# Expert weights in a two-layer mixture-of-experts kernel: 2 MB loads into 16 KB places for six of the eight pairs of experts in each layer

## The chip, the cores and the metric

One core of one Trainium2 chip. The metric is device time in microseconds (us) of one execution. The engines are PE (TensorE, matmul), DVE (VectorE), ACT (ScalarE), POOL (GpSimd) and SP (SyncE, which here only issues transfers); sixteen DMA engines move data between device memory and SBUF. All engines run their own instruction streams in order and wait for one another by semaphores.

## The reference

A first block (a conformer convolution and an MLP) is followed by a second block of two layers. Each of these two layers ends with an expert-choice mixture of experts, and the change is there alone:

```python
def ec_moe(h, w_router, w_gate, w_up, w_down):
    b, n, d = h.shape                                 # 1, 512, 1024
    cap = EC_CAPACITY_FACTOR * n // N_EXPERTS         # 64 tokens for each of 16 experts
    aff = jax.nn.softmax(h.astype(jnp.float32) @ w_router.astype(jnp.float32), axis=-1)
    g, idx = lax.top_k(aff.swapaxes(1, 2), cap)
    xs = jax.vmap(lambda hb, ib: hb[ib])(h, idx)
    a = jax.nn.silu(jnp.einsum('becd,edf->becf', xs, w_gate)) * jnp.einsum('becd,edf->becf', xs, w_up)
    y = jnp.einsum('becf,efd->becd', a, w_down) * g[..., None].astype(h.dtype)
    ...  # the rows of y are added back at the tokens idx
```

Each expert has three 1024 x 1024 float32 matrices (gate, up, down) of 4 MB. Sixteen experts in two layers make 403 MB that have to be read once.

## The kernel before

The kernel is written in a tile language: a program names tiles in pools, and a scheduler derives every semaphore wait from which instruction reads and writes which tile. A pool is a stretch of SBUF; a tile of a tag that has n buffers takes the n buffers in turn, and what writes a buffer waits until the last reader of its former tile is done.

`moe(l)` runs once for each layer. It treats the sixteen experts in eight pairs (j and j + 8, j = 0 to 7): expert j uses the left 64 columns of the PE array and expert j + 8 the right 64. For a pair, `gate_up` makes the gate product and the up product by `product` (L1465), the activation lies between and behind them on ACT and DVE, and `down` transposes the activation, makes the down product and adds the result to the 512 tokens (`combine`, L1534, in layer 0; `add_rows`, L1545, in layer 1). Between these, `gather` and `gather_part` (L1427) pick the next pair's tokens by matmul. From the first pair's down part on, PE's order is held as written.

A product has eight k steps; each takes four matmuls (two halves of 512 columns for each of two experts, L1473). The weights of a step come from a load. `rows` views a matrix as `(p k) n -> p k n`, so that partition p holds rows 8p to 8p + 7, which lie in one run of device memory; two k steps are then 8 KB in one run for each partition, 1 MB over 128 partitions. `product` asks `eload` for such a load for each expert at every second k step, which makes 8 loads to a product and 24 (25.17 million bytes) to a pair. SP issues all of them, in program order, and an SP instruction that waits holds up all loads behind it.

`eplace` gives the SBUF place of a load, from a ring of 14 places of 8 KB a partition: eight pages of the pool `wst` ("p"; tile name w), and the halves of three big buffers, b0, b1 and b3 ("0", "1", "3"; in layer 1 the tensor X stands in for b3). A half-buffer pair is one tile. Two more loads of the first pair go to small tiles (`we`). A place is loaded again when PE has done the products of its former load.

```python
place = "wlwh"[2 * self.ng - 28:2 * self.ng - 26] if self.ng in (14, 15) else \
    "pppppppp001133"[(self.ng - 2 * (self.ng > 15)) % 14]
```

The scheduler gives SP's loads eight completion semaphores in turn (DMAHW0 to DMAHW7), and a load waits until the load before it on its semaphore has landed: at most eight loads are under way.

For the last pair (j = 7), `down_last` (L1560) reads the down matrices in two halves of 512 columns, in loads of 512 KB whose runs are 2 KB (512 float32), so that the first half of the output can be finished while the second is read.

Of the kernel before, what the change touches and what calls it, by code (L numbers as in the profile page):

```python
# [5 lines left out]
F32 = mybir.dt.float32  # L6
# [5 lines left out]
PSUM = bass.MemoryType.PSUM  # L12
# [141 lines left out]
class _Net:  # L154
# [8 lines left out]

    def run(self):
        tc = self.tc
        with tc.tile_pool(name="per", bufs=1) as self.per, \
                tc.tile_pool(name="wst", bufs=8) as self.wst, \
                tc.tile_pool(name="wsp", bufs=4) as self.wsp, \
                tc.tile_pool(name="big", bufs=1) as self.big, \
                tc.tile_pool(name="tmp", bufs=2) as self.tmp, \  # L170
                tc.tile_pool(name="sml", bufs=2) as self.sml, \
                tc.tile_pool(name="dram", bufs=1, space=bass.MemoryType.DRAM) as self.dram:
            self.setup()
            with tc.tile_pool(name="ps", bufs=1, space=PSUM) as self.ps:
                self.block1()
                if self.stop >= 4:
                    self.layer0_proj()
            if self.stop >= 5:
                with tc.tile_pool(name="ps", bufs=1, space=PSUM) as self.ps:
                    self.layer0_attn()  # L180
            with tc.tile_pool(name="ps", bufs=1, space=PSUM) as self.ps:
                if self.stop >= 6:
                    self.mix_out(0, self.a["w_out"], self.oh, self.ol, "gm", last_head=True)
                if self.stop >= 7:
                    self.moe(0)
                if self.stop >= 8:
                    self.layer1_mixer()
                if self.stop >= 9:
                    self.moe(1)

    def pe(self, ins):

# [166 lines left out]
    def beside(self, products):  # L359

        for i, product in enumerate(products[::-1]):
            ins = product()
            if i:
                self.tc.keep_in_program_order(ins)
# [978 lines left out]
    def moe(self, l):  # L1343
        self.ng, self.blk, self.rowwise = 0, None, l == 1
        if self.rowwise:
            self.grow = self.wsp.tile([128, D], F32, name="grow", tag="wl")
            for h in range(2):
                nc = self.nc
                nc.scalar.copy(self.grow[:, 512 * h:512 * h + 512],
                               self.spread(self.fgate[:, 4 * h:4 * h + 4], 4, self.mm_ps()))  # L1350
        self.dump("d_aff%d" % l, self.af)
        after = None
        if l == 0 and self.stop >= 8:
            self.fill(0, "gm1")
            self.g1 = self.gain("m1", self.vec("norm_mix", 8, 8), "sm1")
            after = self.layer1_norm
        gs = self.gather(0)
        self.gather_part(gs, 0, 1)
        self.slots()
        for j in range(8):  # L1360
            act = self.gate_up(l, j, gs[0], (lambda k: self.gather_part(gs, k + 1, 1 + k % 2) if k % 2 or k == 0
                                               else None) if j == 0 else None)
            self.pinned = True
            if j < 7:
                gs = self.gather(j + 1)
                self.gather_part(gs, 0, 4)
            elif l == 0:
                with self.logs_table():
                    self.nc.scalar.copy(self.sml.tile([128, 1], F32, name="done", bufs=1), act[:, 1023:])
            end = j == 7 and l == 1 and self.stop >= 99  # L1370
            self.down(l, j, act, end, after, lambda: self.gather_part(gs, 4, 4))
        self.dump("d_z%d" % l, self.X)
# [61 lines left out]
    def eplace(self):  # L1434
# [12 lines left out]
        t, self.blk = self.blk[:, 2048:], None  # L1447
        return t

    def eload(self, src):  # L1450

        t = self.eplace()
        if isinstance(t, list):
            for k in range(2):
                self.nc.sync.dma_start(t[k], src[:, k])
            return t
        v = t.rearrange("p (k n) -> p k n", k=2)
        self.nc.sync.dma_start(v, src)
        return [v[:, k] for k in range(2)]
# [5 lines left out]
    def product(self, name, l, j, lhs, mid=None):  # L1465

        ps = [self.mm_ps(), self.mm_ps()]
        for k in range(KT):
            if k % 2 == 0:
                w = [self.eload(self.rows(name, l, j + 8 * b)[:, k:k + 2]) for b in range(2)]  # L1470
            for n in range(2):
                for b in range(2):
                    self.pe(self.nc.tensor.matmul(ps[n][64 * b:64 * b + 64], lhs[:, k, 64 * b:64 * b + 64],  # L1473
                                                  w[b][k % 2][:, 512 * n:512 * n + 512],
                                                  start=(k == 0), stop=(k == KT - 1), skip_group_check=True))
            if mid and k < 6:
                mid(k)
        return ps
# [181 lines left out]
```

## Time and profile before

| | |
|---|---|
| median of three runs | 2104.41 us (2100.71, 2104.41, 2108.16) |
| the profiled execution, its own time | 2108.61 us |
| its span, first to last instruction | 2106.8 us, granted PE clock 0.984 |
| busy: PE, PE weight loads, DVE, ACT | 2003.3, 1341.0, 1007.3, 559.0 us |
| expert part of layer 0 | about 939 to 1417 us |
| expert part of layer 1 | about 1635 us to the end |

The profile divides the span into 40 slices of 52.7 us; slices 19 to 26 and 32 to 40 are the expert parts. A busy PE is not PE at its peak: the ends of matmuls are modelled. A float32 matmul is recorded as two instructions, so the 32 matmuls of a product are 64 in the trace. The DMA share of a window is the mean busy share of the sixteen DMA engines; it can read a little above 1, since packets overlap.

### The profile page before, as it was taken

The page shows a single profiled execution, that of the slowest core. Times are in us where ns is not written, and L with a number is a line of the kernel's source. Part 1 is how long each engine was busy: PE and PEld are TensorE (multiplying, and loading weights), DVE is VectorE, ACT ScalarE, POOL GpSimd, SP SyncE. Part 2 cuts the span into 40 slices and gives each one's busy share as a digit, 9 for nine tenths or more (in the row PEclk, how much of TensorE's full clock was granted, in tenths as well). Part 3 has the DMA queues.
Part 4 walks back from the last instruction along what each step waited for, and adds up shares of the span by engine and source line. Part 5 has one row for each costly group of instructions (what it writes and reads, how often), then busy time and mean ns, then how long its engine had stood idle before and what let it go on. Part 6 is the DMA issues. An engine that isn't in the chain of part 4 may idle for free. (4 is left out here: it accounts for less than half of the span.)

```text
span 2106.8 us, 26895 instructions
## 1 busy us (share of the span) xinstructions
PE 2003.3 (95%) x10922; PEld 1341.0 (64%) x10922; DVE 1007.3 (48%) x2004; ACT 559.0 (27%) x1039; POOL 17.2 (1%) x20
## 2 busy tenths in 40 slices
PE   7999999999999989989999999979998999999997
PEld 5759888788888978865444434428887544444442
DVE  4888995887584569661222212225457122222221
ACT  3344624243343359620000000023234000000000
POOL 0000000000000000000000000010000000000000
PEclk9999999999999999989999999989999999999999
DMA  9826484688411254449999999992254899999998
GB/s 362 288 80 231 172 296 160 222 289 244 144 48 41 79 159 114 174 160 374 408 421 421 421 421 421 420 363 81 100 193 161 328 409 422 422 422 422 422 422 327
DMA packets 158955, 582.84 MB, mean 277 GB/s; under 512 B 12593, under 2 KB 21713, under 8 KB 111984
## 3 DMA queue, kind: packets, MB, share of 16 engines
q1 hardware_dynamic: 158352, 580.70, 72.1%
q8 instruction: 86, 1.41, 0.3%
q10 hardware_dynamic: 288, 0.39, 0.1%
q14 instruction: 37, 0.30, 0.0%
q0 software_dynamic: 192, 0.03, 0.0%
HBM read 571.50 MB, written 2.11 MB: 272 GB/s over the span
## 5 line engine op out<-in xcount | busy, mean ns | idle before, releaser
L453 PE MATMUL mm<-b,wh 128*128 128x512 f32 (+1 forms) x2272 | 578.4, 344 | 1.3 <-ACT b L408 0.9
L453 PEld LDWEIGHTS mm<-b,wh 128*128 128x128 f32 x2272 | 394.9, 191 | 61.5 <-issue 6.7
L453 PE MATMUL mm<-b,wl 128*128 128x512 f32 (+1 forms) x1136 | 388.9, 344 | 0.8 <-DVE wl L448 0.8
L1473 PE MATMUL mm<-w,xs 128*64 128x512 f32 x1152 | 262.8, 600 | 12.6 <-DMA w<-w_u 12.6
L448 DVE TENSOR_TENSOR wl<-w,wh 128x1024 fp32r<-128x1024 f32 x160 | 194.0, 1222 | 160.6 <-ACT wh L447 159.4
L447 ACT CAST wh<-w 128x1024 fp32r<-128x1024 f32 x164 | 170.4, 1049 | 316.9 <-PE mm L453 276.3
L453 PEld LDWEIGHTS mm<-b,wl 128*128 128x128 f32 x1136 | 216.2, 191 | 27.9 <-issue 2.5
L1491 DVE TENSOR_TENSOR ea<-mm,ea 128x512 f32<-128x512 f32 x32 | 22.1, 692 | 398.0 <-PE mm L1473 374.6
L1473 PEld LDWEIGHTS mm<-w,xs 128*64 128x64 f32 x1152 | 84.9, 138 | 175.2 <-issue 141.4
L249 DVE SCALAR_TENSOR_TENSOR w<-w,sc 128x512 f32<-128x512 f32 x252 | 184.6, 748 | 3.8
L453 PE MATMUL mm<-wh,b 128*128 128x512 f32 (+1 forms) x640 | 179.1, 363 | 1.0 <-ACT b L408 1.0
L1473 PE MATMUL mm<-b,xs 128*64 128x512 f32 x720 | 166.1, 594 | 4.6 <-DMA b<-w_u 4.5
L1427 PEld LDWEIGHTS sm<-o,b 128*128 128x128 f32 x1024 | 118.9, 194 | 35.1 <-DVE o L1416 16.4
L1427 PE MATMUL sm<-o,b 128*128 128x128 f32 x1024 | 126.4, 281 | 14.2 <-DVE o L1416 14.2
L453 PEld LDWEIGHTS mm<-wh,b 128*128 128x128 f32 x640 | 114.5, 190 | 24.4 <-issue 5.0
L1473 PEld LDWEIGHTS mm<-b,xs 128*64 128x64 f32 x720 | 57.8, 137 | 104.4 <-issue 83.2
L453 PE MATMUL mm<-wl,b 128*128 128x512 f32 (+1 forms) x320 | 115.6, 361 | 0.0
L1473 PE MATMUL mm<-w,eaT 128*64 128x512 f32 x512 | 112.6, 594 | 2.1 <-ACT eaT L1504 2.1
L1487 ACT ACTIVATE ea<-mm 128x512 f32<-128x512 f32 x32 | 19.1, 597 | 321.0 <-PE mm L1473 321.0
L1504 ACT COPY eaT<-mm 128x512 f32<-128x512 f32 x32 | 17.2, 589 | 304.1 <-PE mm L1503 303.8
L1431 DVE TENSOR_SCALAR xs<-sm,fgs 128x128 f32<-128x128 f32 x128 | 44.3, 405 | 109.9 <-PE sm L1427 109.9
L1473 PEld LDWEIGHTS mm<-w,eaT 128*64 128x64 f32 x512 | 36.2, 137 | 72.4 <-issue 68.4
(333 smaller groups left out, 2158.5 us busy)
## 6 DMA issues: line engine op xcount, KB each, us to landing
w<-w_g SPq DMA_DIRECT2D x80, 1024.0 KB, 19.7
w<-w_d SPq DMA_DIRECT2D x64, 1024.0 KB, 18.4
w<-w_u SPq DMA_DIRECT2D x64, 1024.0 KB, 19.7
b<-w_u SPq DMA_DIRECT2D x50, 1024.0 KB, 19.8
w<-ada_w SPq DMA_DIRECT2D x48, 1024.0 KB, 5.3
b<-w_g SPq DMA_DIRECT2D x40, 1024.0 KB, 19.8
b<-w_d SPq DMA_DIRECT2D x40, 1024.0 KB, 19.8
w<-w SPq DMA_DIRECT2D x32, 1024.0 KB, 7.0
```

Source lines behind the costliest of these rows:

```text
L249: nc.vector.scalar_tensor_tensor(acc, w[:, i], sc, acc, op0=ALU.mult, op1=ALU.add)
L447: self.nc.scalar.copy(vh, w[:, i:i + kp])
L448: (lo or self.nc.vector).tensor_tensor(vl, w[:, i:i + kp], vh.bitcast(F32), op=ALU.subtract)
L453: mm = lambda *v, **k: self.pe(self.nc.tensor.matmul(*v, **k))
L1427: self.pe(nc.tensor.matmul(ps[:, 128 * i:128 * i + 128], self.xn[:, t, 128 * k:128 * k + 128], o[:, t], start=(t == 0), stop=(t == 3), ski ...
L1431: nc.vector.tensor_scalar(xs[:, k], ps[:, 128 * i:128 * i + 128], self.fgs[:, 0, k:k + 1], self.fgs[:, 1, k:k + 1], op0=ALU.mult, op1=ALU.add)
L1473: self.pe(self.nc.tensor.matmul(ps[n][64 * b:64 * b + 64], lhs[:, k, 64 * b:64 * b + 64], w[b][k % 2][:, 512 * n:512 * n + 512], start=(k ...
L1487: nc.scalar.activation(av[:, :, 64 * n:64 * n + 64], gp[n].rearrange("p (q k) -> p k q", k=KT), AF.Silu)
L1491: nc.vector.tensor_tensor(av[:, :, c], up[n].rearrange("p (q k) -> p k q", k=KT), av[:, :, c], op=ALU.mult)
L1504: nc.scalar.copy(aT[:, 4 * h:4 * h + 4], ps.rearrange("p (k n) -> p k n", k=4))
```

## The change

From the second pair (j = 1) to the last but one (j = 6) of each layer, `product` takes four k steps in a load (`ewide`): 16 KB in one run for each partition, 2 MB a load, 12 loads to a pair. The ring of places becomes seven places of 16 KB: four tiles of a pool of wide pages, and b0, b1 and b3 (or X) whole. The pool `wst` of eight 8 KB pages is closed ahead of pair 1 and a pool of four 16 KB pages opened in its SBUF; ahead of pair 7 it is changed back. For this the pool is moved to the end of the list of pools, and the conditions on `self.stop`, which all hold in this kernel, are dropped. The first and the last pair are loaded as before.

```diff
--- before.py
+++ after.py
@@ -163,30 +163,32 @@
 
     def run(self):
         tc = self.tc
+        psum = lambda: tc.tile_pool(name="ps", bufs=1, space=PSUM)
         with tc.tile_pool(name="per", bufs=1) as self.per, \
-                tc.tile_pool(name="wst", bufs=8) as self.wst, \
                 tc.tile_pool(name="wsp", bufs=4) as self.wsp, \
                 tc.tile_pool(name="big", bufs=1) as self.big, \
                 tc.tile_pool(name="tmp", bufs=2) as self.tmp, \
                 tc.tile_pool(name="sml", bufs=2) as self.sml, \
-                tc.tile_pool(name="dram", bufs=1, space=bass.MemoryType.DRAM) as self.dram:
+                tc.tile_pool(name="dram", bufs=1, space=bass.MemoryType.DRAM) as self.dram, \
+                contextlib.ExitStack() as last, contextlib.ExitStack() as self.held:
+            self.places(1)
             self.setup()
-            with tc.tile_pool(name="ps", bufs=1, space=PSUM) as self.ps:
+            with psum() as self.ps:
                 self.block1()
-                if self.stop >= 4:
-                    self.layer0_proj()
-            if self.stop >= 5:
-                with tc.tile_pool(name="ps", bufs=1, space=PSUM) as self.ps:
-                    self.layer0_attn()
-            with tc.tile_pool(name="ps", bufs=1, space=PSUM) as self.ps:
-                if self.stop >= 6:
-                    self.mix_out(0, self.a["w_out"], self.oh, self.ol, "gm", last_head=True)
-                if self.stop >= 7:
-                    self.moe(0)
-                if self.stop >= 8:
-                    self.layer1_mixer()
-                if self.stop >= 9:
-                    self.moe(1)
+                self.layer0_proj()
+            with psum() as self.ps:
+                self.layer0_attn()
+            self.ps = last.enter_context(psum())
+            self.mix_out(0, self.a["w_out"], self.oh, self.ol, "gm", last_head=True)
+            self.moe(0)
+            self.layer1_mixer()
+            self.moe(1)
+
+    def places(self, n):
+
+        self.held.close()
+        self.wst = self.held.enter_context(self.tc.tile_pool(name="wst%d" % n, bufs=8 // n))
+        self.wide = n == 2
 
     def pe(self, ins):
 
@@ -1358,6 +1360,8 @@
         self.gather_part(gs, 0, 1)
         self.slots()
         for j in range(8):
+            if j in (1, 7):
+                self.places(2 if j == 1 else 1)
             act = self.gate_up(l, j, gs[0], (lambda k: self.gather_part(gs, k + 1, 1 + k % 2) if k % 2 or k == 0
                                                else None) if j == 0 else None)
             self.pinned = True
@@ -1447,6 +1451,19 @@
         t, self.blk = self.blk[:, 2048:], None
         return t
 
+    def ewide(self, src):
+
+
+        place = "pppppppp001133"[(self.ng - 2) % 14]
+        self.ng += 2
+        if place == "p":
+            t = self.wst.tile([128, 4096], F32, name="w", tag="w")
+        else:
+            t = self.X.rearrange("p f t -> p (f t)") if place == "3" and self.rowwise else self.block(int(place))
+        v = t.rearrange("p (k n) -> p k n", k=4)
+        self.nc.sync.dma_start(v, src)
+        return [v[:, k] for k in range(4)]
+
     def eload(self, src):
 
         t = self.eplace()
@@ -1465,13 +1482,14 @@
     def product(self, name, l, j, lhs, mid=None):
 
         ps = [self.mm_ps(), self.mm_ps()]
+        m, load = (4, self.ewide) if self.wide else (2, self.eload)
         for k in range(KT):
-            if k % 2 == 0:
-                w = [self.eload(self.rows(name, l, j + 8 * b)[:, k:k + 2]) for b in range(2)]
+            if k % m == 0:
+                w = [load(self.rows(name, l, j + 8 * b)[:, k:k + m]) for b in range(2)]
             for n in range(2):
                 for b in range(2):
                     self.pe(self.nc.tensor.matmul(ps[n][64 * b:64 * b + 64], lhs[:, k, 64 * b:64 * b + 64],
-                                                  w[b][k % 2][:, 512 * n:512 * n + 512],
+                                                  w[b][k % m][:, 512 * n:512 * n + 512],
                                                   start=(k == 0), stop=(k == KT - 1), skip_group_check=True))
             if mid and k < 6:
                 mid(k)
```

What the change moves is SP's queue alone: the instructions of PE, DVE, ACT and POOL stand in the same order as before, with other buffer names. Two places of SP's queue follow, both in layer 0; layer 1 has the same. A row is line, operation, tile written <- tensor read, partitions x elements, and the semaphores it waits for (PE_49 is PE's count of done instructions, DMAHW the landings of earlier loads; w is a page, b_ with a number a big buffer, w_g, w_u, w_d the gate, up and down matrices, cut to the name's stem).

SP before, from the fourth load of pair 1 on:

```order
L1458 DMA b_8762<-w_g 128x2048 [waits DMAHW7_49]
L1458 DMA b_8773<-w_g 128x2048 [waits DMAHW0_49,PE_49]
L1458 DMA b_8773<-w_g 128x2048 [waits DMAHW1_49]
L1458 DMA w<-w_g 128x2048 [waits DMAHW2_49,PE_49]
L1458 DMA w<-w_g 128x2048 [waits DMAHW3_49,PE_49]
L1458 DMA w<-w_u 128x2048 [waits DMAHW4_49,PE_49]
L1458 DMA w<-w_u 128x2048 [waits DMAHW5_49,PE_49]
L1458 DMA w<-w_u 128x2048 [waits DMAHW6_49,PE_49]
L1458 DMA w<-w_u 128x2048 [waits DMAHW7_49,PE_49]
L1458 DMA w<-w_u 128x2048 [waits DMAHW0_49,PE_49]
L1458 DMA w<-w_u 128x2048 [waits DMAHW1_49,PE_49]
L1458 DMA b_8836<-w_u 128x2048 [waits DMAHW2_49,PE_49]
```

SP now, from the first load of pair 1 on:

```order
L1464 DMA b_8755<-w_g 128x4096 [waits DMAHW4_49,PE_49]
L1464 DMA b_8757<-w_g 128x4096 [waits DMAHW5_49,PE_49]
L1464 DMA b_8775<-w_g 128x4096 [waits DMAHW6_49,PE_49]
L1464 DMA w<-w_g 128x4096 [waits DMAHW2_49,DMAHW3_49,DMAHW1_49,DMAHW7_49,Activation_sequencer_49,PE_49]
L1464 DMA w<-w_u 128x4096 [waits DMAHW0_49]
L1464 DMA w<-w_u 128x4096 x2
L1464 DMA b_8821<-w_u 128x4096 [waits DMAHW4_49,PE_49]
L1464 DMA b_8887<-w_d 128x4096 [waits DMAHW5_49,PE_49]
L1464 DMA b_8889<-w_d 128x4096 [waits DMAHW6_49,PE_49]
L1464 DMA w<-w_d 128x4096 [waits DMAHW7_49,PE_49]
L1464 DMA w<-w_d 128x4096 [waits DMAHW0_49,PE_49]
```

Before, each page waits for its own PE count, the products of one load of pair 0's down part. Now the first page of the new pool waits once for all eight old pages: its PE count is that of the last product of pair 0's down part, which before only the eighth page (the last w<-w_u row above) waited for. The next three pages have no PE wait left.

SP before, from the last load of pair 6 to the sixth page of pair 7's gate matrices:

```order
L1458 DMA b_10184<-w_d 128x2048 [waits DMAHW3_49]
L1458 DMA b_10255<-w_g 128x2048 [waits DMAHW4_49,PE_49]
L1458 DMA b_10255<-w_g 128x2048 [waits DMAHW5_49]
L1458 DMA w<-w_g 128x2048 [waits DMAHW6_49,PE_49]
L1458 DMA w<-w_g 128x2048 [waits DMAHW7_49,PE_49]
L1458 DMA w<-w_g 128x2048 [waits DMAHW0_49,PE_49]
L1458 DMA w<-w_g 128x2048 [waits DMAHW1_49,PE_49]
L1458 DMA w<-w_g 128x2048 [waits DMAHW2_49,PE_49]
L1458 DMA w<-w_g 128x2048 [waits DMAHW3_49,PE_49]
```

SP now, from the last four loads of pair 6 to the eighth page of pair 7:

```order
L1464 DMA w<-w_d 128x4096 [waits DMAHW1_49,PE_49]
L1464 DMA w<-w_d 128x4096 [waits DMAHW2_49,PE_49]
L1464 DMA b_10067<-w_d 128x4096 [waits DMAHW3_49,PE_49]
L1464 DMA b_10069<-w_d 128x4096 [waits DMAHW4_49,PE_49]
L1475 DMA b_10151<-w_g 128x2048 [waits DMAHW5_49,PE_49]
L1475 DMA b_10151<-w_g 128x2048
L1475 DMA w<-w_g 128x2048 [waits DMAHW6_49,DMAHW1_49,DMAHW7_49,DMAHW0_49,PE_49]
L1475 DMA w<-w_g 128x2048 x3
L1475 DMA w<-w_g 128x2048 [waits DMAHW2_49]
L1475 DMA w<-w_g 128x2048 [waits DMAHW3_49]
L1475 DMA w<-w_u 128x2048 [waits DMAHW4_49]
L1475 DMA w<-w_u 128x2048 [waits DMAHW5_49]
```

Now the first narrow page waits once for all four wide pages: its PE count is that of the first half of pair 6's down product, the half read from the two w<-w_d rows. The seven pages behind it have no PE wait.

## Rows read from the trace of the kernel before

**Rows 1.** Page, the span in 40 slices: DMA share in tenths, then GB/s

```profile
DMA  9826484688411254449999999992254899999998
GB/s 362 288 80 231 172 296 160 222 289 244 144 48 41 79 159 114 174 160 374 408 421 421 421 421 421 420 363 81 100 193 161 328 409 422 422 422 422 422 422 327
```

**Rows 2.** Windows in the expert parts; columns named in the first line

```profile
core 0: us, PE busy (x) PEld busy (x) DVE busy (x) ACT busy (x) POOL busy (x), PEclk, DMA share, GB/s
...
1060.00:1340.00 280.00, 267.41 (x1370) 121.09 (x1370) 57.30 (x107) 16.84 (x28) 0.21 (x1) 1.00 1.01 421
...
1850.00:2050.00 200.00, 190.14 (x976) 89.27 (x974) 47.38 (x88) 11.76 (x20) 0.00 (x0) 1.00 1.01 422
```

**Rows 3.** PE's waits in layer 0's pairs, 1060 to 1385: us, times, longest

```profile
PE mm L1473 <- DMA w<-w_u: 6.6, 5, 1.3
...
PE mm L1473 <- DMA b<-w_u: 3.2, 4, 1.3
```

**Rows 4.** PE's waits in layer 1's pairs, 1640 to 2076

```profile
PE mm L1473 <- DMA w<-w_u: 6.0, 5, 1.4
...
PE mm L1473 <- DMA b<-w_u: 1.3, 1, 1.3
PE mm L1473 <- DMA X<-w_u: 1.2, 1, 1.2
```

**Rows 5.** Chain of waits in layer 1: start us, us, engine, tile, line, count

```profile
1680.22 13.95 PE mm L1473 x64
...
1701.61 27.64 PE mm L1473 x128
...
1735.69 13.95 PE mm L1473 x64
...
1757.06 27.67 PE mm L1473 x128
...
1833.20 19.86 DMA b<-w_d
```

**Rows 6.** SP's queue in layer 0, pair 0 to 1: start, us, line, load, count

```profile
989.93 0.81 SPq L1458 DMA_DIRECT2D w<-w_g  x2
993.37 7.67 SPq L1458 DMA_DIRECT2D w<-w_u  x6
1011.25 0.80 SPq L1458 DMA_DIRECT2D b<-w_u  x2
```

**Rows 7.** SP's queue in layer 1, same place

```profile
1683.90 0.80 SPq L1458 DMA_DIRECT2D w<-w_g  x2
1687.34 7.67 SPq L1458 DMA_DIRECT2D w<-w_u  x6
1705.23 0.80 SPq L1458 DMA_DIRECT2D b<-w_u  x2
```

**Rows 8.** Windows in which the DMA share falls, layer 0, then layer 1

```profile
1008.00:1016.00 8.00, 8.00 (x40) 2.73 (x38) 3.05 (x6) 0.00 (x0) 0.00 (x0) 1.00 0.88 334
...
1704.00:1708.00 4.00, 4.00 (x20) 1.29 (x18) 0.53 (x2) 0.00 (x0) 0.00 (x0) 1.00 0.76 254
```

**Rows 9.** Window of layer 1's last down matrices, runs of 2 KB

```profile
2076.00:2088.00 12.00, 10.20 (x47) 4.14 (x46) 2.35 (x4) 1.69 (x3) 0.00 (x0) 1.00 1.05 387
```

**Rows 10.** Page, DMA queues: packets, MB, share of 16 engines; loads to landing us

```profile
q8 instruction: 86, 1.41, 0.3%
...
w<-w_g SPq DMA_DIRECT2D x80, 1024.0 KB, 19.7
```

**Rows 11.** PE in layer 0's last pair: start, us, what, [idle before]

```profile
1379.74 3.65 PE L1473 MATMUL mm<-b,xs 128*64 128x512 f32 x14 [1.34 <-DMA b<-w_u]
1384.24 1.09 PE L1503 MATMUL mm<-cs,ea 128*128 128x128 f32 x8 [0.85 <-DVE ea L1491]
1387.72 9.74 PE L1568 MATMUL mm<-w,eaT 128*64 128x512 f32 x32 [2.39 <-ACT eaT L1504]
```

**Rows 12.** Window there, with the granted PE clock

```profile
1384.00:1392.00 8.00, 5.37 (x18) 2.11 (x20) 0.19 (x1) 2.55 (x4) 0.00 (x0) 0.64 1.06 388
```

## The prediction

> **What bounds the kernel now.** I read the slices of the page first, for where the DMA engines are full; then windows inside those stretches; then PE's waits there; then the chain of waits; then SP's queue at the places where the change touches it.
>
> The slices show two plateaus of 420 to 422 GB/s, one in each expert part [rows 1]. Windows inside them give a DMA share of 1.01 at 421 and 422 GB/s, while PE too is 95% busy [rows 2]. So two engines run nearly level, and it has to be settled which one ends last. A pair is 25.17 million bytes, which at 422 GB/s is 59.6 us. A pair costs PE, where it waits for no weights, 1757.06 - 1701.61 = 55.45 us [rows 5]. The loads are the slower, but they enter each part with the ring of fourteen places already filled, so PE meets the stream late. Its waits for loads come to 6.6 + 3.2 = 9.8 us in layer 0 and 6.0 + 1.3 + 1.2 = 8.5 us in layer 1, no single one over 1.4 us [rows 3, 4]; the last of them, 1.34 us, stands before the last step of layer 0's last up product [rows 11]. In both layers the stream of loads therefore sets the end, and PE is only some 9 us behind as a bound. A microsecond lost in the stream is lost in the time; gained, it is worth at most those 9 us a layer.
>
> **The change part by part.** Six pairs of twelve loads make 72 wide loads in a layer in place of 144 narrow ones. The bytes, and what PE, DVE, ACT and POOL do, stay.
>
> *The rate.* No row shows a weight load with runs of 16 KB. Rows show runs of 8 KB at 422 GB/s [rows 2] and of 2 KB at 387 GB/s [rows 9]. For one of sixteen engines that is 8192 x 16 / 422 = 310.6 ns a run and 2048 x 16 / 387 = 84.7 ns. The difference, 225.9 ns for 6144 bytes, is 36.8 ns for a thousand bytes; what is left is 84.7 - 75.3 = 9.4 ns a run that do not depend on its length. By this line a 16 KB run takes 611.8 ns, a 2 MB load (eight runs on each engine) 4.894 us, and two loads of 1 MB at 422 GB/s take 4.970 us: 0.076 us gained, a rate of 428.5 GB/s. Bounds: nothing, if such a run is cut in two or if the 9.4 ns belong to something else; 0.151 us, if the whole constant vanished (the slope alone, 435.7 GB/s). A loss I leave out, though one row looks like it: the instruction fetches are 86 packets in 1.41 MB, 16.4 KB each, and 0.3% of sixteen engines' 2106.8 us is 1.2 us each [rows 10], twice the line. [...] I take the line, since both of its points are rates of this very queue.
>
> [...]
>
> *The drain at pair 1.* The loads now queue in this order: b0, b1 and b3 (or X) whole, then a wide page that waits for all eight old pages. Up to there the places, bytes and waits are those of before, so the DMA engines run dry at the same moment. Before, the first page was issued at 989.93 in layer 0 and 1683.90 in layer 1, when the first quarter of the down product was done, and the other six behind it as PE freed them [rows 6, 7]. Now the first one goes when the down product has ended, at 1680.22 + 13.95 = 1694.17 [rows 5]; in layer 0 when the last two of the six went, 993.37 + 7.67 - 0.80 = 1000.24. That is 10.3 us later in both layers. Nothing is queued on SP that could go in the meantime, and no load is under way: 10.3 us of an idle stream.
>
> Part of it comes back at once. Before, the stream ran dry a second time, before the b<-w_u loads at 1011.25 and 1705.23 [rows 6, 7]: the windows there have 334 GB/s over 8 us and 254 over 4 us [rows 8], which at 422 GB/s is 1.7 and 1.6 us lost. Now four wide pages go together and last 4 x 4.9 = 19.6 us, to about 1715; b0 is free when pair 1's first gate half is done, 1701.61 + 27.64 / 4 = 1708.5. So this second hole closes. Net loss: 10.3 - 1.6 = 8.7 us a layer. PE does not stand still meanwhile: the loads it needs next, b0, b1 and X, have landed, and the first wide page lands at about 1701, seven microseconds before its turn. The price shows up later, when PE meets the delayed stream: 8.7 / (59.6 - 55.45), some two pairs earlier than now.
>
> *The gain on the rest.* Three of the 72 wide loads come before the drain, and what they gain ends in it. 69 x 0.076 = 5.2 us a layer.
>
> *Steady state.* PE frees two 2 MB places every four k steps, 27.64 / 4 = 6.9 us after they land at the latest when it is not behind; its breaks are 1735.69 - (1701.61 + 27.64) = 6.4 us before the down product and 1757.06 - (1735.69 + 13.95) = 7.4 us behind it [rows 5]. A place must be loaded again before the other six have landed, 6 x 4.9 = 29 us. 6.9 + 7.4 is half of that: no new hole. With a pair at 12 x 4.894 = 58.7 us against PE's 55.45, PE remains the faster. That at most eight loads are under way (8 x 1.0486 MB / 422 GB/s = 19.9 us, the step in the chain [rows 5] and the 19.7 us to landing [rows 10]) no longer binds, since there are seven places.
>
> *The change back at pair 7.* The first narrow page waits for the first half of pair 6's down product. Counted from the landing of that half, the half of up before it is done 9.8 - 6.9 = 2.9 us earlier, the break of 6.4 us follows, then 13.95 / 2 = 7.0 us of products: 10.5 us. Queued behind are two wide loads and two narrow ones, 9.8 + 5.0 = 14.8 us. The wait is covered by 4.3 us, less what lies between an issue and its first byte. Cost: nothing; if PE is later than that, each microsecond costs one.
>
> *Sum.* 10.3 - 1.6 - 5.2 = 3.5 us slower in each layer, 7.0 us in all. Against the profiled execution's own 2108.61 us that is 2115.6 us. The median of the runs shown is 4.2 us lower, 2104.41; on it the sum is 2111.4 us, 0.33% slower.
>
> **The rivals.**
>
> *A, the wide runs bring little or nothing.* Then 8.7 us a layer stand, 17.4 us in all: 2121.8 us. For it: no row has such a load. Against it: from 2 to 8 KB the rate rose as a constant per run would have it. [...]
>
> *B, not slower.* The constant vanishes altogether, or lies per load and not per run, with the rate at the slope: 69 x 0.151 = 10.4 us gained a layer against 8.7, 2104.41 - 3.4 = 2101.0 us. It decides from a gain of 8.7 / 69 = 0.126 us a load, or 433 GB/s in the steady windows. More than that can hardly come of it, since PE then becomes the bound within 9 us a layer. Against it: the bound itself is the steepest reading of two windows.
>
> [...]
>
> *D, pair 7's change of pools is not covered*: 2 us or more in each layer, 2115.4 us or above.
>
> **How the numbers follow.** A difference of 0.3% (6.3 us) is about what a measurement of this kernel tells from none. My forecast has 0.50, its own range 2108 to 2115; as it lies at that edge, 0.30 of this counts as slower and 0.20 as the same. A has 0.20, all slower. B has 0.15: 0.10 the same, 0.05 faster. C has 0.12: 0.11 the same, 0.01 faster. D has 0.03, slower. Together: slower 0.53, same 0.41, faster 0.06. The range for 8 in 10 runs from B's 2101 to just below A's far end, 2121.
>
> **What would show it.** Right: in the profile after, windows of the steady stretches at about 428 GB/s; the first w<-w_g load of 2 MB issued some 10 us later against the end of pair 0's up product than before, and the DMA share near zero for somewhat over 10 us there; PE's waits for loads starting some two pairs earlier than now, as one of about 9.8 - 6.9 = 2.9 us in a pair and not three of 1.3; no hole at pair 7. Wrong: 422 GB/s in these windows (A), 433 or more (B), a hole at pair 7 (D), or DMA never idle at pair 1, which would take the whole 8.7 us away.

## The result and the profile after

The changed kernel takes 2115.99 us (median of 7 runs, 2114.11 to 2121.35) against 2105.61 (median of 7 runs, 2100.71 to 2108.16). The medians are 10.4 us apart; over all runs the ratio is 1.0058, 95% interval 1.0044 to 1.0071, so 9 to 15 us slower. The forecast was 7 us slower, 2111.4 us; its sign and range held, the size was low. The profiled execution is the median run, 2115.99 us, span 2114.2, granted clock 0.983.

The page's slices of after (DMA share in tenths, GB/s), against [rows 1]:

```profile
DMA  9826584778311354547999999992254799999998
GB/s 361 287 80 234 185 286 152 242 277 244 133 48 41 85 162 118 179 152 317 429 426 429 427 427 428 405 361 75 100 217 149 311 382 428 428 428 428 428 408 328
```

Windows of after (the changed kernel), columns as in [rows 2]: two in the steady stretches, three over the drain of layer 0 (in pair 0's down product and just after it) and three over layer 1's pair 7.

```profile
1060.00:1300.00 240.00, 226.87 (x1153) 103.69 (x1153) 51.03 (x95) 14.57 (x24) 0.00 (x0) 0.99 1.01 428
1850.00:2000.00 150.00, 142.81 (x749) 68.25 (x750) 37.81 (x72) 9.31 (x16) 0.00 (x0) 1.00 1.01 428
...
988.00:994.00 6.00, 6.00 (x30) 2.01 (x28) 0.00 (x0) 0.00 (x0) 0.00 (x0) 1.00 0.01 5
994.00:1000.00 6.00, 6.00 (x34) 2.55 (x31) 1.02 (x2) 1.37 (x2) 0.00 (x0) 1.00 0.09 19
1000.00:1006.00 6.00, 6.00 (x40) 5.39 (x39) 3.71 (x8) 0.00 (x0) 0.00 (x0) 1.00 0.95 377
...
2038.00:2040.00 2.00, 2.00 (x12) 0.72 (x10) 0.00 (x0) 0.00 (x0) 0.00 (x0) 1.00 0.81 336
2040.00:2042.00 2.00, 2.00 (x12) 0.66 (x10) 0.00 (x0) 0.00 (x0) 0.00 (x0) 1.00 0.47 197
2042.00:2044.00 2.00, 2.00 (x12) 0.63 (x10) 0.00 (x0) 0.00 (x0) 0.00 (x0) 1.00 0.91 270
```

Three things are to be read here; a hole is a stretch in which the DMA engines have too little to do. The steady rate is 428 GB/s, as the line through 2 and 8 KB runs gave it. From 988 to 1000 almost nothing moves (5 and 19 GB/s): the drain. And at pair 7, where the forecast had no hole, there is one, worth 2.2 us at 428 GB/s ((92 + 231 + 158) x 2 / 428). Layer 0 has the same at 1342 to 1348.

SP's queue of after at the drain, against [rows 6]:

```profile
968.34 7.20 SPq L1464 DMA_DIRECT2D b<-w_g  x3
999.00 0.33 SPq L1464 DMA_DIRECT2D w<-w_g  x1
999.38 1.47 SPq L1464 DMA_DIRECT2D w<-w_u  x3
1013.45 0.33 SPq L1464 DMA_DIRECT2D b<-w_u  x1
```

Counted from the start of pair 0's down product (985.00, before 986.25), the first page goes at 14.0 us in place of 3.7: 10.3 us later, the forecast's number. The three pages behind it go at once, and these four loads of 2 MB keep the DMA engines busy until b0 is free (1013.45; 1004 to 1012 read 406 and 446 GB/s), so the second hole of [rows 8] has closed.

PE's waits for loads of after, in layer 1's pairs; rows are start, us, what, [idle before]:

```profile
1782.81 7.08 PE L1491 MATMUL mm<-w,xs 128*64 128x512 f32 x30 [2.43 <-DMA w<-w_u]
1841.46 0.64 PE L1491 MATMUL mm<-w,xs 128*64 128x512 f32 x1 [2.13 <-DMA w<-w_u]
1900.13 7.08 PE L1491 MATMUL mm<-b,xs 128*64 128x512 f32 x30 [0.44 <-DMA b<-w_u]
1950.16 7.09 PE L1491 MATMUL mm<-w,xs 128*64 128x512 f32 x32 [0.36 <-DMA w<-w_u]
1960.16 7.08 PE L1491 MATMUL mm<-w,xs 128*64 128x512 f32 x30 [2.91 <-DMA w<-w_u]
2018.90 8.78 PE L1491 MATMUL mm<-w,xs 128*64 128x512 f32 x30 [2.22 <-DMA w<-w_u]
```

Before, PE first waited in pair 5 and last in pair 7. Now it first waits in pair 2, and in pairs 2, 3, 5 and 6 it waits for 2.1 to 2.9 us at a time. The last wait is in pair 6: **after the hole at pair 7, PE waits for no load any more**, in either layer. The half product at 2018.90 takes 8.78 us where the same 7.08 are the rule; so does the one at 1841.46, which the chain of waits gives whole, and two in layer 0. The granted clock there, in two windows of after:

```profile
1145.00:1151.00 6.00, 6.00 (x22) 1.83 (x24) 0.00 (x0) 0.00 (x0) 0.00 (x0) 0.72 1.00 426
1841.00:1847.00 6.00, 5.54 (x18) 1.75 (x20) 0.00 (x0) 0.00 (x0) 0.00 (x0) 0.72 0.99 423
```

It is 0.72 over 6 us in both, and also in the windows at the other two halves (1322 to 1328, 2018.9 to 2024.9). Only part of such a half ran slower: from 1146.51 to 1149.07 its matmuls start, two at a time, 0.85 us apart, from 1149.65 on 0.43. Each half lost 1.70 us (8.78 against 7.08).

To compare kernels I use marks instead of whole spans, because the part ahead of the experts, whose instructions no edit changes, ended up to 7 us apart from run to run. A layer is counted from the start of its pair 0's down product to the start of the long product behind it (layer 0) or to the end of the span (layer 1). The marks that [rows 5] does not have, and the landing of pair 6's last up load, in before (PE rows, then the chain):

```profile
986.25 13.95 PE L1473 MATMUL mm<-w,eaT 128*64 128x512 f32 x64 [0.24 <-ACT eaT L1504]
1319.91 3.65 PE L1473 MATMUL mm<-w,xs 128*64 128x512 f32 x14 [1.31 <-DMA w<-w_u]
2013.18 3.65 PE L1473 MATMUL mm<-w,xs 128*64 128x512 f32 x14 [1.32 <-DMA w<-w_u]
```

```profile
1435.82 81.89 PE mm L453 x426
```

The same in after:

```profile
985.00 13.95 PE L1491 MATMUL mm<-w,eaT 128*64 128x512 f32 x64 [0.24 <-ACT eaT L1522]
1322.67 8.78 PE L1491 MATMUL mm<-w,xs 128*64 128x512 f32 x30 [2.28 <-DMA w<-w_u]
```

```profile
1438.28 81.93 PE mm L455 x426
1681.80 13.95 PE mm L1491 x64
```

| us in the profiled run | layer 0 | layer 1 | against before |
|---|---|---|---|
| before | 449.6 | 426.6 | |
| after | 453.3 | 432.4 | +3.7, +5.8 |
| pools only | 458.3 | 434.8 | +8.7, +8.2 |
| two loads a place | 456.8 | 434.9 | +7.3, +8.3 |
| wide ahead of pair 0 | 446.8 | 425.6 | -2.8, -1.0 |
| and kept in layer 1 | 446.8 | 425.2 | -2.7, -1.4 |
| drain, kept in layer 1 | 453.3 | 430.6 | +3.7, +4.0 |
| wide blocks only | 449.8 | 428.1 | +0.2, +1.5 |
| pair 1's gate narrow | 445.6 | 422.7 | -4.0, -3.9 |
| and gather in the wait | 446.2 | 423.0 | -3.4, -3.6 |

Each row is one profiled run. Layer 0 is the same code in after and in "drain, kept in layer 1", and in the two rows "wide ahead of pair 0" and "and kept in layer 1"; each of these two couples agrees within 0.1 us.

### The profile page after: what moved, and what is told of

It is laid out like the page before. It is cut to its first block, busy times and chain, and to the rows that moved or that the text cites. A ratio compares the mean times of both kernels' runs of the same rounds, so it can differ in the third digit from the quotient of the medians.

```text
span 2114.2 us, 26652 instructions
## 1 busy us (share of the span) xinstructions
PE 2009.3 (95%) x10922; PEld 1345.3 (64%) x10922; DVE 1007.1 (48%) x2004; ACT 558.5 (26%) x1039; POOL 17.2 (1%) x20
## 3 DMA queue, kind: packets, MB, share of 16 engines
q8 instruction: 86, 1.41, 0.3%
## 5 line engine op out<-in xcount | busy, mean ns | idle before, releaser
L1491 PE MATMUL mm<-w,xs 128*64 128x512 f32 x1152 | 311.2, 610 | 20.5 <-DMA w<-w_u 20.5
L1491 PEld LDWEIGHTS mm<-w,xs 128*64 128x64 f32 x1152 | 97.8, 140 | 200.3 <-issue 159.7
L1491 PE MATMUL mm<-b,xs 128*64 128x512 f32 x720 | 206.9, 596 | 1.0 <-DMA b<-w_u 1.0
L1491 PE MATMUL mm<-w,eaT 128*64 128x512 f32 x512 | 140.2, 594 | 2.1 <-ACT eaT L1522 2.1
L1491 PEld LDWEIGHTS mm<-b,xs 128*64 128x64 f32 x720 | 71.7, 137 | 86.4 <-issue 73.1
L1491 PE MATMUL mm<-b,eaT 128*64 128x512 f32 x320 | 98.3, 594 | 1.3 <-ACT eaT L1522 1.3
```

## The experiments

All were timed beside the kernel before, the first four on one chip and the last four on another (its median there 2105.07 and 2105.68). The diffs are excerpts.

**Pools only.** From the changed kernel: no wide loads, and one change of pools.

```diff
-            if j in (1, 7):
-                self.places(2 if j == 1 else 1)
+            if j == 1:
+                self.places(1)
```

> The loads are those of the kernel before (1 MB, runs of 8 KB); only the pool of eight 8 KB pages is closed and opened again ahead of pair 1, in both layers. My theory (the change of pools drains the queue of loads at pair 1, 8.7 us a layer net): 17.4 us slower than before, a ratio of about 1.008; the DMA engines idle for about 10 us at the end of pair 0's down product, steady windows at 422 GB/s. Rival (the drain is caught up later, since PE is only some 9 us a layer behind the loads, and it is the coarse 2 MB places that made the changed kernel slower): within 3 us of before, with the same idle stretch.

Measured: 2122.51 us, ratio 1.0089 (1.0071 to 1.0108). Windows at the drain and the last wait of layer 1:

```profile
984.00:988.00 4.00, 4.00 (x22) 1.36 (x20) 0.00 (x0) 0.00 (x0) 0.00 (x0) 1.00 0.48 199
988.00:996.00 8.00, 8.00 (x40) 2.59 (x36) 0.00 (x0) 0.28 (x1) 0.00 (x0) 1.00 0.01 2
996.00:1000.00 4.00, 4.00 (x35) 3.54 (x32) 1.50 (x2) 1.10 (x2) 0.00 (x0) 1.00 0.58 205
```

```profile
2085.89 3.65 PE L1491 MATMUL mm<-X,xs 128*64 128x512 f32 x14 [1.23 <-DMA X<-w_u]
```

Steady windows read 422 GB/s. The change of pools by itself costs 8.7 and 8.2 us a layer; nothing is caught up, and PE still waits for the loads in pair 7. This shows the forecast's 8.7 us.

**Two loads a place.** From the changed kernel:

```diff
-        self.nc.sync.dma_start(v, src)
+        for h in range(2):
+            self.nc.sync.dma_start(v[:, 2 * h:2 * h + 2], src[:, 2 * h:2 * h + 2])
```

> The changed kernel with its 16 KB places and both changes of pools, but each place is filled by two loads of 1 MB with runs of 8 KB. My theory (two drains of 8.7 us and two holes of 2.2 us at pair 7 cost 21.8 us, and the 16 KB runs gave 5.2 us a layer of it back): without the runs the whole cost stands, 18 to 22 us slower than before, a ratio of about 1.009 to 1.010, steady windows at 422 GB/s. Rival (the runs give nothing, the rate of 428 GB/s comes from somewhere else, such as the fewer loads or the seven places): the same as the changed kernel, about 1.006, at 428 GB/s.

Measured: 2126.57 us, ratio 1.0100 (1.0081 to 1.0119). Windows over pair 7 of layer 0 and in layer 1's steady stretch:

```profile
1340.00:1350.00 10.00, 9.76 (x58) 4.90 (x59) 1.37 (x4) 1.07 (x2) 0.00 (x0) 1.00 1.01 419
1850.00:2000.00 150.00, 140.94 (x715) 64.62 (x712) 30.27 (x58) 8.70 (x15) 0.00 (x0) 0.98 1.01 422
```

With 8 KB runs the gain is gone, so the rate does not come from the seven places. Run length and load size changed together here; but a constant per load instead of per run, fitted to the rates of the 512 KB and 1 MB loads (387 and 422 GB/s), would give 442 GB/s for 2 MB, an estimate, and 428 was measured. The total is as expected, the reason is not: by the marks the layers cost 7.3 and 8.3 us, not 10.9 each, and there is no hole at pair 7 (from 1340 to 1362 no window falls under 410). The profiled spans differ by 18.1 us (2124.9 and 2106.8): 15.6 in the layers, 3.4 ahead of the experts, -0.9 between the layers.

**Wide pages opened ahead of pair 0.** The drain goes, since pair 1's wide page waits for its own former tile alone.

```diff
+        self.places(2)
         for j in range(8):
-            if j in (1, 7):
-                self.places(2 if j == 1 else 1)
+            self.wide = 1 <= j < 7
+            if j == 7:
+                self.places(1)
...
-        if place == "p":
+        if place == "p" and not self.halved:
             return self.page()
         if self.blk is None:
+            if place == "p":
+                self.blk = self.wst.tile([128, 4096], F32, name="w", tag="w")
+                return self.blk[:, :2048]
```

> As the changed kernel, but the wide pages are opened ahead of pair 0 (whose narrow loads take their halves), so that pair 1's first wide page waits for its own former tile alone; the change back at pair 7 stays in both layers. My theory (drain 8.7, hole at pair 7 2.2, gain of the runs 5.2 us a layer): the drain goes, -5.2 + 2.2 = 3.0 us a layer, about 6 us faster than before, a ratio of about 0.997; no idle stretch at pair 1, the hole at pair 7 still there. Rival (coarse places and the clock that falls behind the lumped waits cost the time, not the drain): about as the changed kernel, 1.005.

Measured: 2102.45 us, ratio 0.9992 (0.9980 to 1.0003). 13 us of the changed kernel's time are gone (by the marks 6.5 and 6.8), which settles the drain against the rival. But 6 us under before were expected and about 2 came, which the interval does not tell from none. The windows of this kernel say why:

```profile
1004.00:1008.00 4.00, 4.00 (x19) 2.31 (x19) 4.00 (x7) 0.00 (x0) 0.00 (x0) 1.00 1.05 451
1008.00:1012.00 4.00, 4.00 (x20) 1.29 (x18) 1.86 (x4) 0.00 (x0) 0.00 (x0) 1.00 0.43 184
1012.00:1016.00 4.00, 4.00 (x22) 1.40 (x20) 0.00 (x0) 0.00 (x0) 0.00 (x0) 1.00 0.37 111
```

Without the drain the second hole is open again and larger: 5.2 us lost (244 + 317, x 4 / 428) where [rows 8] has 1.7. The dip ahead of pair 1's first page is some 1 us larger too (984 to 992: 2.7 us lost, before 1.8). A wide load into b0 needs half of pair 1's gate product done, a narrow one a quarter, 27.64 / 8 = 3.5 us earlier [rows 5].

**And kept to the end of layer 1.**

```diff
-            if j == 7:
+            if j == 7 and l == 0:
```

> As the one with the wide pages opened ahead of pair 0, and in layer 1 they are kept to the end: no change back at its pair 7. My theory (the change back makes the hole of about 2.2 us): 2 us faster than that one, some 8 us faster than before, a ratio of about 0.996; no hole at layer 1's pair 7, that of layer 0 still there. Rival (the hole comes from wide loads that land late and together, whatever the pools): the hole stays in layer 1 and the time is the same as with the change back, 0.997.

Measured: 2102.59 us, ratio 0.9992 (0.9982 to 1.0002): no faster. The same window of layer 1 with the change back, then without:

```profile
2028.00:2032.00 4.00, 4.00 (x20) 1.29 (x18) 0.00 (x0) 0.00 (x0) 0.00 (x0) 1.00 0.89 344
2028.00:2032.00 4.00, 4.00 (x22) 1.36 (x20) 0.00 (x0) 0.00 (x0) 0.00 (x0) 1.00 1.01 426
```

The hole did go, but layer 1 gained only 0.4 us. So half of my theory stands: the change back makes the hole, but the hole costs next to nothing.

**The drain, without the change back in layer 1.** The kernel of the run above, with its change of pools at pair 1:

```diff
-        self.places(2)
         for j in range(8):
+            if j == 1:
+                self.places(2)
```

> The changed kernel with its change of pools ahead of pair 1 in both layers, but in layer 1 the wide pages are kept to the end (pair 7's narrow loads take their halves), so that only layer 1's hole at pair 7 goes. My theory after the first runs (behind the last up product of pair 6 PE is late by more than the loads, waits for no load again, and the hole costs nothing; what costs is the 2 MB grain and the clock that falls behind the long waits): layer 1 lasts as in the changed kernel, 432.4 us from the start of pair 0's down product to the end, against 426.6 before; ratio about 1.005. Rival (the hole is on the path, as the prediction priced it): 2.2 us less in layer 1, 430.2 us.

Measured: 2116.18 us, ratio 1.0050 (1.0033 to 1.0067); layer 1 lasts 430.6 us (span 2116.5). That total is the rival's, but the reason is not. Layer 1's mark, the half product after its last wait and pair 7's gate and up products, from the chain:

```profile
1685.95 13.95 PE mm L1497 x64
...
2023.22 7.09 PE mm L1497 x30
...
2058.15 27.84 PE mm L1497 x128
```

Pair 6's last up load lands 337.3 us behind the mark, in after 337.1. The half product behind it takes 7.09 us and not 8.79, and from its end to the end of the kernel it is 86.2 us against 86.5. So 1.7 of the 1.9 us are the clock (here 1.00 from 2024 to 2028, in after 0.72 from 2018.9 to 2024.9), and at most 0.3 the hole; pair 7's gate and up products take 27.84 here and 28.19 in after, which is where that little lies.

In this kernel the last half is fast though the one before it was slow:

```profile
1964.61 8.78 PE L1497 MATMUL mm<-w,xs 128*64 128x512 f32 x30 [1.93 <-DMA w<-w_u]
2023.22 7.08 PE L1497 MATMUL mm<-w,xs 128*64 128x512 f32 x30 [0.42 <-DMA w<-w_u]
```

In after it is the other way round: 7.08 at 1960.16, then a wait of 2.22 and 8.78 at 2018.90. Pairs 3 and 4 show the same: the wait is 0.41 or 0.44 us after a slow half and 2.13 or 2.14 after a fast one. So PE's next wait for loads takes up what a slow half lost; only the one after the last wait lengthens the layer.

**Wide blocks only.** No change of pools; b0, b1 and b3 or X by wide loads, page units by two narrow ones.

```diff
-            t = self.wst.tile([128, 4096], F32, name="w", tag="w")
+            ws = []
+            for h in range(2):
+                v = self.page().rearrange("p (k n) -> p k n", k=2)
+                self.nc.sync.dma_start(v, src[:, 2 * h:2 * h + 2])
+                ws += [v[:, k] for k in range(2)]
+            return ws
```

> No change of pools: the pool of eight 8 KB pages stays, products go in units of four k steps, the three big blocks take one load of 2 MB and each page unit two of 1 MB: 31 wide loads a layer instead of 72. Rate alone (rival): 31 x 0.076 = 2.3 us less a layer, 0.998 of before. My theory (a unit of four k steps frees its block 3.4 us later, which opens a hole at pair 1, and leaves PE half a product after the last landing of pair 6's up product instead of a quarter, 3.4 us, of which the waits in pair 7 give back about as much, with 1.7 us lost where the clock falls): +1 to +3 us a layer, 1.001 to 1.003 of before.

Measured: 2108.86 us, ratio 1.0019 (1.0006 to 1.0032), 424 GB/s in the steady windows. The rate rose and the time did too, as expected from the grain (the size of the unit in which places come free and products wait). By the marks the layers cost +0.2 and +1.5 us where +1 to +3 each were expected, so layer 0 came out below. The 57 GB/s in 1008 to 1012 are its hole at pair 1.

**Pair 1's gate product narrow** (from the kernel kept wide to the end of layer 1, which the expectation calls the last run):

```diff
-        m, load = (4, self.ewide) if self.wide else (2, self.eload)
+        m, load = (4, self.ewide) if self.wide and (j, name) != (1, "w_g") else (2, self.eload)
```

> The wide pages opened ahead of pair 0 and kept to layer 1's end, as in the last run, and the gate product of pair 1 still in loads of 1 MB, so that b0 comes free after a quarter of it and not after a half. My theory: the second hole at pair 1 (in the last run 111 and 180 GB/s in two windows of 4 us, 5.3 us lost; before 1.7 us) shrinks by 3.4 us a layer, PE's long waits with it: 4 to 7 us less than that run, 0.996 to 0.9975 of before. Rival (PE's own work is the bound there already): the same as that run, 0.999.

Measured: 2099.02 us, ratio 0.9969 (0.9956 to 0.9983): **faster than both kernels**, 0.3% below the kernel before and within the range expected. The hole at pair 1 and layer 1's last wait:

```profile
1008.00:1012.00 4.00, 4.00 (x22) 1.43 (x20) 1.26 (x3) 0.00 (x0) 0.00 (x0) 1.00 0.70 229
1012.00:1016.00 4.00, 4.00 (x22) 1.29 (x18) 0.00 (x0) 0.00 (x0) 0.00 (x0) 1.00 1.00 426
```

```profile
2003.89 7.08 PE L1496 MATMUL mm<-w,xs 128*64 128x512 f32 x30 [1.56 <-DMA w<-w_u]
```

1.9 us are lost there instead of 5.3. Of these 3.4 us a layer, 1.3 and 2.5 reach the end of the layers. The half product after layer 1's last wait takes 7.08 us here.

**Gather in the wait.** As that one; `gate_up` passes a hook to the up product:

```diff
+    def ahead(self, gs, j, k):
+        if k == 1:
+            gs.append(self.gather(j + 1))
+        if k == 3:
+            self.gather_part(gs[0], 0, 4)
```

> As the one with pair 1's gate product narrow, and from pair 1 to pair 6 the first half of the next pair's gather (32 matmuls, 3.84 us) is moved from behind the up product to its middle, where PE waits for the second half's loads. My theory: the gather covers the wait, no up half takes 8.8 us any more, and PE is 1.7 to 4 us earlier behind pair 6 in each layer; the loads bound both layers: 2 to 5 us less than without the move, about 0.995 of before. Rival (the loads bound it already, the waits and the clock behind them are covered): the same as without the move.

Measured: 2099.43 us, ratio 0.9968 (0.9955 to 0.9981): the same as without the move, so the rival holds. The long waits are gone as meant:

```profile
1944.21 3.65 PE L1506 MATMUL mm<-w,xs 128*64 128x512 f32 x16
1947.80 3.84 PE L1443 MATMUL sm<-o,b 128*128 128x128 f32 x32
1951.57 7.09 PE L1506 MATMUL mm<-w,xs 128*64 128x512 f32 x32
```

The up half behind the gather takes 7.09 us, no wait for a load is over 1.4 us, and layer 1's last one has moved into pair 6's down product (1.3 us at 2029.03). So up to the last wait the loads bind this kernel, and covering PE's waits buys nothing there. Nor was there a slow half to win back: without the move the half after the last wait had already run in 7.08 us, in both layers.

## Why the prediction was right in sign and low in size

**Rate: right.** 428 GB/s against 428.5; two loads a place put it back to 422. One constant per run, 9.4 ns by the line, fits 2, 8 and 16 KB (387, 422 and 428 GB/s).

**Drain: right.** 10.3 us later, second hole closed, and 8.7 and 8.2 us a layer when it stands alone.

**The stream up to pair 6: right.** 65 wide loads behind the drain land by then: 8.7 - 65 x 0.076 = 3.8 us later. Measured 337.67 - 333.66 = 4.01 in layer 0 and 337.10 - 332.96 = 4.14 in layer 1.

**The sum's last step, from the stream to the end of the layer: wrong.** The forecast took the stream of loads to set the end of each layer ("a microsecond lost in the stream is lost in the time") and added rate and drain to the end. In the changed kernel the stream binds only as far as pair 6's up product; from there PE's own work sets the end. Three terms were missing, read between the same marks. A wide unit leaves PE half a product after the last landing and not a quarter: 7.08 - 3.65 = +3.43 us. The clock that falls after the long wait (0.72 from 2018.9 to 2024.9): 8.78 - 7.08 = +1.70. And PE's waits of pair 7, which are gone, with what else is shorter from there to the end: in layer 1 86.52 us instead of 89.97, -3.45, of which 2.6 are the waits; in layer 0 106.83 instead of 112.26, -5.43, of which 2.9 are the waits. Together 4.14 + 3.43 + 1.70 - 3.45 = 5.82 in layer 1 and 4.01 + 3.43 + 1.70 - 5.43 = 3.71 in layer 0. Layer 0's agreement with the forecast's 3.5 is thus luck: the missing terms, +5.1 and -5.4, cancel there. The two layers give 9.5 of the 10.4 us between the medians; the rest lies within what the part ahead of the experts varies from run to run.

**Pair 7's change of pools: wrong as a step, without effect.** "The wait is covered by 4.3 us" failed: a hole of 2.2 us opened in both layers, as rival D has it. Pair 6's up half took 8.78 us where 6.9 were counted, which is 1.9 of the 4.3. The cover was short by more than that: with the wide pages opened ahead of pair 0 the same half takes 7.08 us and the rate still falls to 344 GB/s over 4 us. What the rest is stays open. The hole takes both the change back and loads of 2 MB; without the one (kept to the end of layer 1, 426 GB/s there) or the other (two loads a place, 419) there is none. But D's price failed too: the hole lies where PE waits for no load, and taking it away in layer 1 left the time as it was. In layer 0 it was not taken away; there too PE waits for no load after it.

**The rivals.** A is out by 428 GB/s, B by the same rows (433 were needed). C, that layer 0 absorbs its delay behind the last up step, holds in part: its 32 matmuls of the last down product now take 8.78 us at a granted clock of 0.79 (1388 to 1396), before 9.74 [rows 11] at 0.64 [rows 12]; this 1.0 us lies in the 5.43 above. The wait of 2.39 us stays:

```profile
1391.49 8.78 PE L1586 MATMUL mm<-w,eaT 128*64 128x512 f32 x32 [2.39 <-ACT eaT L1522]
```

**Coarse waits.** They were to begin two pairs earlier, as one of 2.9 us; they began three pairs earlier, with 2.1 to 2.9 us. That the clock falls after some of them, to 0.72 over 6 us, was not foreseen.

## What to carry to other kernels

Closing and reopening a pool turns separate releases of pages into one barrier: price it as the time from the first release to the last (here 10.3 us), and open the pool where its pages are idle anyway. Longer runs saved a constant for each run here, 9.4 ns, which two rates of the same queue gave well (428.5 GB/s forecast, 428 measured), but the larger load also coarsened what is released and what the consumer waits for (3.43 us behind the last landing), so follow the last unit through the consumer to the end, not just the stream. Time that the consumer loses ahead of a wait is taken up by that wait (here 0.41 or 0.44 us after a slow half, 2.13 or 2.14 after a fast one); only what it loses after its last wait counts (1.7 us). Compare variants between marks inside the trace; a total that matches a theory can come from another term.

## What the hardware showed unexpectedly

The granted clock fell (0.72 over 6 us) after some of PE's single waits of 2 to 3 us in an otherwise busy stretch, though not after each: in the changed kernel's layer 1 the waits of 2.43 and 2.91 us left the next half product at 7.08 us, those of 2.13 and 2.22 us were followed by 8.78. In the kernel with the drain but without the change back the same loads were followed by slow halves at other pairs (8.78, 8.77 and 8.78 us at 1787, 1904 and 1965, and not the last, 7.08). Before, with waits of at most 1.41 us, one quarter of the sixteen that waited took 4.00 us in place of 3.65, at a granted clock of 1.00 (1948.3 to 1952.3). Which waits are hit is open.
